# The end of the global attention and the second output product: order by token halves, a weight split moved, the last tile in halves

## The chip, the cores and the metric

One core of a Trainium2 chip runs one layer in one launch. The metric is the device time in microseconds: three timed runs of the kernel before gave 1565.99, 1567.54 and 1567.87, median 1567.54. Engines: PE (TensorE, matmuls, and PEld, its weight loads), DVE (VectorE), ACT (ScalarE), POOL (GpSimd), SP (SyncE, which here issues nearly all DMAs).

## The reference

One layer over 1024 tokens of width 1024, with 256 context tokens. Two attention branches run side by side, A windowed and B global, each with 8 query heads of 64 and 2 key heads; their outputs are merged through gates, projected and added to the stream, and a convolutional SwiGLU follows.

```
h = x * (1 + scale1) + shift1
q, k, v, gate_logits = h @ w_in + b_in             # rotary, RMS norm on q and k of B
o_a = windowed_attention(...); o_b = global_attention(...)     # softmax over keys and context
g_a, g_b = split(sigmoid(gate_logits))
y = (g_a * (o_a @ w_branch_a) + g_b * (o_b @ w_branch_b)) @ w_out
x = layer_norm(alpha * x + gate1 * y)
x = layer_norm(alpha * x + gate2 * conv_ffn(x * (1 + scale2) + shift2))
```

The change touches the end of `o_b`, the product `o_b @ w_branch_b` and the merge ahead of `w_out`.

## The kernel before, in words

All tensors are float32, and PE multiplies in a rounded 32-bit form. To keep precision each operand is **split** into a high part (a rounded copy, "h") and a low part (the difference, "l"); a product is then three matmuls (`mm3`, lines 88 to 91: high by high, high by low, low by high). The function `split` (lines 80 to 86) makes the two parts, each on an engine that the caller names.

The stages in order: modulation and projections (to about 330 us), the 16 units of branch A (to 485), the 16 units of branch B (to 757), the output product of B with the merge (to 805), `w_out` and the first LayerNorm (to about 885), the FFN's up tiles (to 1330), its down tiles (to 1552) and the last LayerNorm.

**A unit** is 128 queries of one key group, with four heads side by side: a name such as `1_7_1` is branch 1 (B), query tile 7, group 1, the last of all. After its softmax come the value steps: for each of ten key tiles n PE transposes the probabilities (`ptr`, L613), the result is split into `pth` and `ptl`, and two matmuls add to `av` (L634, L635). The split is made by ACT (cast, L622) and DVE (subtraction, L623); for the key tiles in `POOL_LO`, 2 and 6 of branch B, ACT copies to `prw` (L619) and POOL makes both parts (L83, L86), and the matmuls of such a tile are queued one place later (`PLAG`). When `av` is complete, `out_step` copies it to `avs` (ACT, L640), moves its upper half down (`up`, POOL, L642), adds the halves (`ot`, L646: POOL in branch B, DVE in A), multiplies by the broadcast reciprocal of the softmax sums (`rb`, L649, POOL) and splits into the `O` tiles (POOL, L83 and L86).

**The output product of B** has eight tiles f of 128 channels by 1024 tokens, each for two token halves of 512 (hf). Half 0 is made of query tiles 0 to 3, half 1 of 4 to 7, so only half 1 needs the last unit. A half is 12 matmuls, 24 a tile. Its weight comes in four pieces for two tiles each (`wb`), each loaded into `rwb` and split into `hwb` and `lwb`. Tiles 0 and 1 are made by `branch_steps` (L947 evicts with the gate as factor into `bT1_f`), four groups in the order (0, half 0), (0, half 1), (1, half 0), (1, half 1), in the PSUM tiles `pt` of the attention, one bank each. Tiles 2 to 7 follow in a loop of their own (evicted at L1086), each in a `big` tile of two banks; there are three such buffers. Tile 2 needs the weight piece `wb[1]`, which is loaded and split after tiles 0 and 1. The function `merge` adds the tile to that of branch A (L1067, DVE), casts (`mh`, ACT) and subtracts (`ml`, DVE). Then `w_out`'s product y reads `mh` and `ml` (first y: tokens 0 to 511), again in `big` tiles, as do the first up tiles of the FFN, named u0_j and u1_j.

After up tile 2 the `big` tiles are given up, and the up tiles from 3 on use the eight PSUM banks singly, in a fixed order of banks (`PSU` = 6, 7, 2, 3, 4, 5, 0, 1) for a, b, c, d of each tile. So the third bank in use is one that a `big` tile held, and its first matmul waits until that tile's last reader is done.

The order on PE is the order of the code. On ACT, DVE and POOL the compiler's scheduler may move instructions, except inside `manual_schedule`, where the code's order holds. Each engine takes its queue in order, and so does SP with its DMAs.

Of the kernel before, what the change touches and what calls it, by code (L numbers as in the profile page):

```python
# [68 lines left out]
def layer_kernel(  # L69
# [393 lines left out]
    class Unit:  # L463
# [141 lines left out]
        def value_steps(self):  # L605
            nm, kt = self.id, self.kt
            vh = self.br * 2 + self.g
            parts = {}

            def tr_step(n):  # L610
                tr = pt_tile(f"ptr{nm}_{n}")
                for h in range(4):
                    nc.tensor.transpose(tr[:, h * P:(h + 1) * P], self.pslice(h, n), ident)  # L613
                hi = att.tile([P, 512], R32, tag="pth", name=f"pth{nm}_{n}", bufs=4)
                lo = att.tile([P, 512], R32, tag="ptl", name=f"ptl{nm}_{n}", bufs=4)
                pooled = n in POOL_LO[self.br]
                if pooled:
                    rw = att.tile([P, 512], F32, tag="ptr", name=f"prw{nm}_{n}", bufs=2)
                    nc.scalar.copy(rw, tr)  # L619
                    split(rw, hi, lo, nc.gpsimd, nc.gpsimd)  # L620
                else:
                    nc.scalar.copy(hi, tr)  # L622
                    nc.vector.tensor_tensor(out=lo, in0=tr, in1=hi.bitcast(F32), op=ALU.subtract)  # L623
                parts[n] = hi, lo
                return pooled

            def av_step(n):
                first = self.left == len(kt)
                self.left -= 1
                if first:  # L630
                    self.av = ps2.tile([P, 512], F32, tag="av", name=f"av{nm}")
                hi, lo = parts.pop(n)
                v = VT[kt[n] // 2][:, kt[n] % 2, vh]
                nc.tensor.matmul(self.av, v, hi, start=first, stop=False)  # L634
                nc.tensor.matmul(self.av, v, lo, start=False, stop=self.left == 0)  # L635

            def out_step():
                av = self.av
                avs = att.tile([P, 512], F32, tag="ptr", name=f"avs{nm}", bufs=2)
                nc.scalar.copy(avs, av)  # L640
                up = att.tile([HD, 512], F32, tag="up", name=f"up{nm}", bufs=1)
                nc.gpsimd.tensor_scalar(out=up, in0=avs[HD:P], scalar1=1.0, scalar2=0.0, op0=ALU.mult, op1=ALU.add)  # L642
                ot = att.tile([P, 2, P], F32, tag="ot", name=f"ot{nm}", bufs=1)
                oe = nc.gpsimd if self.br else nc.vector
                for h in range(2):
                    oe.tensor_tensor(out=ot[h * HD:(h + 1) * HD],  # L646
                                     in0=avs[0:HD].rearrange("p (a b q) -> p a b q", b=2, q=P)[:, :, h],
                                     in1=up.rearrange("p (a b q) -> p a b q", b=2, q=P)[:, :, h], op=ALU.add)
                nc.gpsimd.tensor_tensor(out=ot, in0=ot, in1=self.rb, op=ALU.mult)  # L649
# [247 lines left out]
    def s_tile(name):  # L897
        return ps2.tile([P, T], F32, tag="s", name=name, bufs=2)

    def p_tile(name):  # L900
        return att.tile([P, T], F32, tag="p", name=name, bufs=8)

# [21 lines left out]
    def branch_steps(br, wsrc, halves, wpool, engs, f2s=range(4)):  # L924
# [24 lines left out]
        for f2 in f2s:  # L949
            steps.append(lambda f2=f2: ld(f2, f"{f2}_{halves[0]}"))  # L950
            for f in (2 * f2, 2 * f2 + 1):
                for hf in halves:
                    steps.append(lambda f=f, hf=hf: grp(f, hf, pt_tile))
        return steps

    def done(br, i, g):
# [40 lines left out]
    nc.sync.dma_start(cvw, conv)  # L997
    nc.sync.dma_start(cvb, convb)
    hput("KC", *[f"VT{t}" for t in range(5)])
    for st_ in first[1:]:  # L1000
        st_()
    ps2.release()
    att.release()
    qp.release()
# [13 lines left out]

    def sml(name, w=512):
        return ps3.tile([P, w], F32, tag="sml", name=name, bufs=2)  # L1020

    def weight(src, nm, n=8, tag="w", he=None, le=None, rtag="raw"):
        if rtag:
            r = post.tile([P, 8, P], F32, tag=rtag, name=f"r{nm}", bufs=3)[:, 0:n]
        else:
            r = ht(f"r{nm}", (P, n, P))
            hput(f"r{nm}")
        nc.sync.dma_start(r, src)
        if tag is None:
            h, l = (ht(f"{a}{nm}", (P, n, P), R32) for a in "hl")  # L1030
        else:
            pool = wq if tag == "w" else post
            h, l = (pool.tile([P, 8, P], R32, tag=tag, name=f"{a}{nm}", bufs=4)[:, 0:n] for a in "hl")
        split(r, h, l, he or nc.gpsimd, le or nc.gpsimd)
        return h, l

    def hsl(hf):
        return slice(hf * HALF, (hf + 1) * HALF)
# [23 lines left out]
            nc.sync.dma_start(z, xT[f][:, hsl(hf)])  # L1062
            nc.gpsimd.tensor_scalar(out=z, in0=z, scalar1=ALPHA, scalar2=0.0, op0=ALU.mult, op1=ALU.add)

    def merge(f):
        m = bT[0, f]
        nc.vector.tensor_tensor(out=m, in0=m, in1=bT[1, f], op=ALU.add)  # L1067
        mh, ml = ht(f"mh{f}", dt=R32), ht(f"ml{f}", dt=R32)
        split(m, mh, ml, nc.scalar, nc.vector)
        hput(f"bT0_{f}", f"bT1_{f}")  # L1070
        mrg.append((mh, ml))

    for f in (0, 1):
        merge(f)
    wb = {f2: weight(w_b[f2], f"wb{f2}", 8, he=nc.scalar, le=nc.vector, rtag=None) for f2 in (1, 2)}
    for f in range(2, KT):
        bT[1, f] = ht(f"bT1_{f}")
        nc.sync.dma_start(bT[1, f], sgd[KT + f])
        w = wb[f // 2]
        ps = big(f"b1_{f}")  # L1080
        for j in range(4):
            k = (f % 2) * 4 + j
            for hf in (0, 1):
                a = O[1, hf, 0, j // 2][:, j % 2], O[1, hf, 1, j // 2][:, j % 2]
                mm3(ps[:, hsl(hf)], (w[0][:, k], w[1][:, k]), a, j == 0, j == 3)
# [823 lines left out]
```

## Time and profile before

| | before |
|---|---|
| timed runs, us | 1565.99, 1567.54, 1567.87 |
| profiled execution, us | 1568.55 |
| its span, first to last instruction, us | 1566.8 |
| mean granted TensorE clock | 0.995 |

Busy time is what the profile counts between start and end of an instruction, so overlapping matmuls leave a busy PE even where they start later than they could. In the rows of the timeline the columns are start, duration, engine, line, operation, output and inputs, shape, and in brackets the engine's idle time before it and the instruction that ended it. In the rows by stretch the columns are busy time and number of instructions on PE, PEld, DVE, ACT and POOL, the granted clock of PE, the share of DMA engines busy and the GB/s.

### The profile page before, as it was taken

What the parts mean: (1) busy time and instruction counts of PE and PEld (TensorE: products, weight loads), DVE (VectorE), ACT (ScalarE), POOL (GpSimd) and SP (SyncE); (2) the same over time, 40 slices, a digit from 0 to 9 for tenths busy, and PEclk for the clock granted to TensorE, in tenths of its full rate; (3) what the DMA queues carried; (4) which work ended last, traced back from release to release, by engine and by line L of the source; (5) the groups of instructions that cost most, each with busy time, mean ns of one, the idle gap of its engine ahead of it and who ended that gap; (6) DMA issues with size and microseconds to landing.
All of it is one profiled execution on the core that took longest, in us unless ns stands there. A gap on an engine that the chain in (4) does not pass through costs nothing.

```text
span 1566.8 us, 22288 instructions
## 1 busy us (share of the span) xinstructions
PE 1533.8 (98%) x7804; PEld 1283.3 (82%) x7804; DVE 1187.2 (76%) x1707; ACT 808.2 (52%) x1430; POOL 788.7 (50%) x801
## 2 busy tenths in 40 slices
PE   9999999999999999999999999999999999999997
PEld 7888888888877878877788998888888888888887
DVE  6676976548887777778573789888888888657884
ACT  5323223358887777777330574544444444435552
POOL 0356423526667777776442445766677774021121
PEclk9999999999999999999999999999999999999998
DMA  9776662322236666631550223233334446996721
GB/s 370 263 245 238 210 239 93 109 82 64 65 118 142 143 161 148 142 75 32 180 178 24 82 91 112 93 108 109 121 108 112 113 115 187 365 269 208 254 103 55
DMA packets 113105, 232.11 MB, mean 148 GB/s; under 512 B 13056, under 2 KB 27904, under 8 KB 112896
## 3 DMA queue, kind: packets, MB, share of 16 engines
q1 hardware_dynamic: 97760, 201.82, 38.2%
q0 software_dynamic: 10400, 20.19, 8.3%
q10 hardware_dynamic: 4832, 8.68, 1.5%
q8 instruction: 61, 1.00, 0.3%
q14 instruction: 52, 0.43, 0.1%
HBM read 179.45 MB, written 65.86 MB: 157 GB/s over the span
## 4 chain that ended last, share of the span: by engine, by line
PE 56%; DVE 2%; ACT 1%; issue 0%; POOL 0%; DVEq 0%; ACTq 0%
PE p L91 4%; PE p L89 4%; PE p L90 4%; PE b L91 3%; PE b L89 2%; PE b L90 2%; PE c L89 2%; PE a L89 2%; PE d L89 2%; PE d L91 2%; PE a L90 2%; PE c L90 2%; PE d L90 2%; PE a L91 2%; PE c L91 2%; PE y L90 2%
## 5 line engine op out<-in xcount | busy, mean ns | idle before, releaser
L623 DVE TENSOR_TENSOR ptl<-ptr,pth 128x512 fp32r<-128x512 f32 x188 | 124.9, 683 | 32.5 <-ACT pth L622 32.1
L622 ACT CAST pth<-ptr 128x512 fp32r<-128x512 f32 x188 | 106.8, 592 | 52.7 <-PE ptr L613 31.2
L86 DVE TENSOR_TENSOR ld<-rd,hd 128x1024 fp32r<-128x1024 f32 x77 | 95.9, 1264 | 50.0 <-ACT hd L81 47.9
L505 ACT ACTIVATE p<-p,nm 128x1024 f32<-128x1024 f32 (+2 forms) x128 | 125.9, 985 | 4.6 <-DVE p L538 4.3
L613 PE MATMUL ptr<-ident,p 128*128 128x128 f32 x816 | 122.2, 276 | 4.4 <-DVE ptl L623 3.2
L81 ACT CAST hd<-rd 128x1024 fp32r<-128x1024 f32 x77 | 79.4, 1050 | 81.5 <-PE p L91 51.3
L613 PEld LDWEIGHTS ptr<-ident,p 128*128 128x128 f32 x816 | 94.0, 140 | 25.7 <-DVE ptl L623 7.7
L86 POOL TENSOR_TENSOR wlg<-wg,whg 128x512 fp32r<-128x512 f32 x32 | 46.5, 1462 | 123.6 <-ACT whg L81 123.3
L634 PE MATMUL av<-pth,VT 128*128 128x512 f32 x236 | 104.4, 442 | 2.7 <-ACT avs L640 1.5
L89 PE MATMUL p<-hd 128*128 128x512 f32 x264 | 103.4, 392 | 0.0
L91 PE MATMUL p<-hd,ld 128*128 128x512 f32 x264 | 102.9, 390 | 0.0
L90 PE MATMUL p<-ld,hd 128*128 128x512 f32 x264 | 102.9, 390 | 0.0
L635 PE MATMUL av<-ptl,VT 128*128 128x512 f32 x236 | 98.3, 416 | 3.5 <-POOL ptl L86 3.5
L89 PE MATMUL g<-hh,whg 128*128 128x512 f32 x256 | 100.0, 391 | 0.0
L91 PE MATMUL g<-hh,wlg 128*128 128x512 f32 x256 | 99.8, 390 | 0.0
L90 PE MATMUL g<-hl,whg 128*128 128x512 f32 x256 | 99.7, 390 | 0.0
L538 DVE TENSOR_SCALAR_CACHE_REDUCE p<-s,cvt,nmc 128x1024 f32<-128x1024 f32 x64 | 83.2, 1316 | 8.7 <-PE s L494 7.6
L493 PE MATMUL s<-KL,q 128*128 128x512 f32 (+2 forms) x192 | 75.8, 395 | 5.5 <-ACT p_x L505 2.8
L494 PE MATMUL s<-KL,q 128*128 128x512 f32 (+2 forms) x192 | 71.6, 373 | 0.0
L786 ACT ACTIVATE sg<-g,bgc 128x512 f32<-128x512 f32 x32 | 22.0, 686 | 96.1 <-PE g L91 96.1
L81 ACT CAST wS<-s 128x512 fp32r<-128x512 f32 x76 | 45.3, 620 | 45.3 <-POOL s L1211 44.6
L81 ACT CAST wA<-ru 128x512 fp32r<-128x512 f32 x57 | 35.5, 623 | 63.7 <-PE d L91 34.9
(436 smaller groups left out, 5030.2 us busy)
## 6 DMA issues: line engine op xcount, KB each, us to landing
wml<-in_wmodT_dram SPq DMA_DIRECT2D x48, 512.0 KB
ru<-in_w_up_dram SPq DMA_DIRECT2D x38, 512.0 KB
rd<-td SPq DMA_DIRECT2D x55, 256.0 KB
rd<-sd SPq DMA_DIRECT2D x44, 256.0 KB
rd<-in_w_dn_dram SPq DMA_DIRECT2D x33, 256.0 KB
wm<-in_wmodT_dram SPq DMA_DIRECT2D x16, 512.0 KB
wg<-in_w_g_dram SPq DMA_DIRECT2D x32, 256.0 KB
sgd<-sg ACTq DMA_DIRECT2D x32, 256.0 KB
```

Source lines behind the costliest of these rows:

```text
L81: nc.scalar.copy(hi, src)
L86: lo_eng.tensor_tensor(out=lo, in0=src, in1=hi.bitcast(F32), op=ALU.subtract)
L89: nc.tensor.matmul(ps, a[0], b[0], start=start, stop=False, skip_group_check=resumed)
L90: nc.tensor.matmul(ps, a[0], b[1], start=False, stop=False, skip_group_check=resumed)
L91: nc.tensor.matmul(ps, a[1], b[0], start=False, stop=stop, skip_group_check=resumed)
L505: nc.scalar.activation(p, s, AF.Exp, bias=nm[:, h:h + 1], scale=scale, accum_out=sm[:, h:h + 1])
L538: nc.vector.tensor_scalar(out=p, in0=o, scalar1=self.qscale(nqs)[:, hs] if self.br else -1.0, scalar2=self.other[:, hs], op0=ALU.mult, op1 ...
L613: nc.tensor.transpose(tr[:, h * P:(h + 1) * P], self.pslice(h, n), ident)
L622: nc.scalar.copy(hi, tr)
L623: nc.vector.tensor_tensor(out=lo, in0=tr, in1=hi.bitcast(F32), op=ALU.subtract)
L634: nc.tensor.matmul(self.av, v, hi, start=first, stop=False)
L635: nc.tensor.matmul(self.av, v, lo, start=False, stop=self.left == 0)
```

## The change

Four edits, in one diff:

1. In the last unit no key tile is split on POOL, and its `ot` is added on DVE.
2. The groups of tiles 0 and 1 are called in the order (0, half 0), (1, half 0), (0, half 1), (1, half 1), and the last of them takes an `s` tile of PSUM, not a `pt`.
3. `wb[1]` is called between the first and the second group, inside a `manual_schedule` of DVE and ACT with them; its buffers are given back after tile 3. The function `weight` moves up with it, as do the lines that follow it unchanged.
4. Tile 7 is computed, evicted and merged in two halves, in `sml` tiles of PSUM in place of a `big` one.

```diff
@@ value_steps, tr_step, out_step
+            last = self.id == f"1_{NT - 1}_1"
...
-                pooled = n in POOL_LO[self.br]
+                pooled = n in POOL_LO[self.br] and not last
...
-                oe = nc.gpsimd if self.br else nc.vector
+                oe = nc.gpsimd if self.br and not last else nc.vector
...
+    def s_half(name):
+        return s_tile(name)[:, 0:HALF]
...
@@ branch_steps
                 for hf in halves:
-                    steps.append(lambda f=f, hf=hf: grp(f, hf, pt_tile))
+                    mk = s_half if br and f % 2 and hf else pt_tile
+                    steps.append(lambda f=f, hf=hf, mk=mk: grp(f, hf, mk))
...
-    for st_ in first[1:]:
-        st_()
+    wb = {}
+    with tc.manual_schedule(engines={mybir.EngineType.DVE, mybir.EngineType.Activation}):
+        first[1]()
+        wb[1] = weight(w_b[1], "wb1", 8, tag=None, he=nc.scalar, le=nc.vector, rtag=None)
+        for n in (3, 2, 4):
+            first[n]()
...
-    def merge(f):
+    def merge(f, parts=(slice(0, T),)):
         m = bT[0, f]
-        nc.vector.tensor_tensor(out=m, in0=m, in1=bT[1, f], op=ALU.add)
         mh, ml = ht(f"mh{f}", dt=R32), ht(f"ml{f}", dt=R32)
-        split(m, mh, ml, nc.scalar, nc.vector)
+        for s in parts:
+            nc.vector.tensor_tensor(out=m[:, s], in0=m[:, s], in1=bT[1, f][:, s], op=ALU.add)
+            split(m[:, s], mh[:, s], ml[:, s], nc.scalar, nc.vector)
...
-    wb = {f2: weight(w_b[f2], f"wb{f2}", 8, he=nc.scalar, le=nc.vector, rtag=None) for f2 in (1, 2)}
+    wb[2] = weight(w_b[2], "wb2", 8, he=nc.scalar, le=nc.vector, rtag=None)
...
-        ps = big(f"b1_{f}")
-        for j in range(4):
-            k = (f % 2) * 4 + j
-            for hf in (0, 1):
-                a = O[1, hf, 0, j // 2][:, j % 2], O[1, hf, 1, j // 2][:, j % 2]
-                mm3(ps[:, hsl(hf)], (w[0][:, k], w[1][:, k]), a, j == 0, j == 3)
-        nc.vector.tensor_tensor(out=bT[1, f], in0=ps, in1=bT[1, f], op=ALU.mult)
-        merge(f)
+        halves = [(0, 1)] if f < KT - 1 else [(0,), (1,)]
+        for hs in halves:
+            n = HALF * len(hs)
+            b = bT[1, f][:, hs[0] * HALF:hs[0] * HALF + n]
+            ps = big(f"b1_{f}") if len(hs) == 2 else sml(f"b1_{f}_{hs[0]}")
+            for j in range(4):
+                k = (f % 2) * 4 + j
+                for m, hf in enumerate(hs):
+                    a = O[1, hf, 0, j // 2][:, j % 2], O[1, hf, 1, j // 2][:, j % 2]
+                    mm3(ps[:, hsl(m)], (w[0][:, k], w[1][:, k]), a, j == 0, j == 3)
+            nc.vector.tensor_tensor(out=b, in0=ps, in1=b, op=ALU.mult)
+        merge(f, [slice(hs[0] * HALF, (hs[-1] + 1) * HALF) for hs in halves])
         if f == 3:
+            hput("hwb1", "lwb1")
             wb[3] = weight(w_b[3], "wb3", 8, he=nc.scalar, le=nc.vector, rtag=None)
```

Below the first edit the lines of the changed kernel are one higher than before, in the output product some four to sixteen.

What stands on POOL at the end of the last two units (`_7_0_` and `_7_1_`), before:

```order
L83 TENSOR_SCALAR pth1_7_1_2_8635<-prw1_7_1_2_8637 128x512
L642 TENSOR_SCALAR up1_7_0_8654<-avs1_7_0_8652 64x512
L86 TENSOR_TENSOR ptl1_7_1_2_8636<-prw1_7_1_2_8637,pth1_7_1_2_8635 128x512
L646 TENSOR_TENSOR ot1_7_0_8656<-avs1_7_0_8652,up1_7_0_8654 64x256 x2
L649 TENSOR_TENSOR ot1_7_0_8656<-ot1_7_0_8656,rb1_7_0_8537 128x256
L83 TENSOR_SCALAR O1100_7333<-ot1_7_0_8656 128x2x128
L86 TENSOR_TENSOR O1110_7334<-ot1_7_0_8656,O1100_7333 128x2x128
L83 TENSOR_SCALAR pth1_7_1_6_8698<-prw1_7_1_6_8700 128x512
L86 TENSOR_TENSOR ptl1_7_1_6_8699<-prw1_7_1_6_8700,pth1_7_1_6_8698 128x512
L642 TENSOR_SCALAR up1_7_1_8749<-avs1_7_1_8747 64x512
L646 TENSOR_TENSOR ot1_7_1_8751<-avs1_7_1_8747,up1_7_1_8749 64x256 x2
L649 TENSOR_TENSOR ot1_7_1_8751<-ot1_7_1_8751,rb1_7_1_8687 128x256
```

and on POOL now:

```order
L643 TENSOR_SCALAR up1_7_0_8652<-avs1_7_0_8650 64x512
L647 TENSOR_TENSOR ot1_7_0_8654<-avs1_7_0_8650,up1_7_0_8652 64x256 x2
L650 TENSOR_TENSOR ot1_7_0_8654<-ot1_7_0_8654,rb1_7_0_8537 128x256
L83 TENSOR_SCALAR O1100_7333<-ot1_7_0_8654 128x2x128
L86 TENSOR_TENSOR O1110_7334<-ot1_7_0_8654,O1100_7333 128x2x128
L643 TENSOR_SCALAR up1_7_1_8745<-avs1_7_1_8743 64x512
L650 TENSOR_TENSOR ot1_7_1_8747<-ot1_7_1_8747,rb1_7_1_8687 128x256
L83 TENSOR_SCALAR O1101_7566<-ot1_7_1_8747 128x2x128
L86 TENSOR_TENSOR O1111_7567<-ot1_7_1_8747,O1101_7566 128x2x128
```

The four splits of key tiles 2 and 6 and the last unit's two additions are gone from POOL; the first go to ACT and DVE, the additions to DVE.

What stands on DVE from the last subtraction of the attention on (`bT1_f` are evictions and then merges into `bT0_f`), before:

```order
L623 TENSOR_TENSOR ptl1_7_1_9_8734<-ptr1_7_1_9_8728,pth1_7_1_9_8733 128x512
L947 TENSOR_TENSOR bT1_0_8759<-b1_0_0_8761,bT1_0_8759 128x512
L947 TENSOR_TENSOR bT1_0_8759<-b1_0_1_8776,bT1_0_8759 128x512
L1067 TENSOR_TENSOR bT0_0_5576<-bT0_0_5576,bT1_0_8759 128x1024
L947 TENSOR_TENSOR bT1_1_8790<-b1_1_0_8792,bT1_1_8790 128x512
L86 TENSOR_TENSOR ml0_8835<-bT0_0_5576,mh0_8834 128x1024
L947 TENSOR_TENSOR bT1_1_8790<-b1_1_1_8807,bT1_1_8790 128x512
L1067 TENSOR_TENSOR bT0_1_5717<-bT0_1_5717,bT1_1_8790 128x1024
L86 TENSOR_TENSOR lwb1_8846<-rwb1_8843,hwb1_8845 128x1024
L86 TENSOR_TENSOR lwb2_8852<-rwb2_8849,hwb2_8851 128x1024
L86 TENSOR_TENSOR ml1_8840<-bT0_1_5717,mh1_8839 128x1024
L1086 TENSOR_TENSOR bT1_2_8855<-b1_2_8857,bT1_2_8855 128x1024
```

and now:

```order
L624 TENSOR_TENSOR ptl1_7_1_9_8730<-ptr1_7_1_9_8724,pth1_7_1_9_8729 128x512
L647 TENSOR_TENSOR ot1_7_1_8747<-avs1_7_1_8743,up1_7_1_8745 64x256 x2
L951 TENSOR_TENSOR bT1_0_8757<-b1_0_0_8759,bT1_0_8757 128x512
L86 TENSOR_TENSOR lwb1_8776<-rwb1_8773,hwb1_8775 128x1024
L951 TENSOR_TENSOR bT1_1_8779<-b1_1_0_8781,bT1_1_8779 128x512
L951 TENSOR_TENSOR bT1_0_8757<-b1_0_1_8796,bT1_0_8757 128x512
L1079 TENSOR_TENSOR bT0_0_5576<-bT0_0_5576,bT1_0_8757 128x1024
L951 TENSOR_TENSOR bT1_1_8779<-b1_1_1_8811,bT1_1_8779 128x512
L86 TENSOR_TENSOR ml0_8839<-bT0_0_5576,mh0_8838 128x1024
L1079 TENSOR_TENSOR bT0_1_5717<-bT0_1_5717,bT1_1_8779 128x1024
L86 TENSOR_TENSOR lwb2_8851<-rwb2_8848,hwb2_8850 128x1024
L86 TENSOR_TENSOR ml1_8844<-bT0_1_5717,mh1_8843 128x1024
```

`lwb1` has moved six rows up, ahead of the second group's eviction, and `ot` has come in. Its high part, `hwb1`, now stands on ACT directly behind `avs1_5_1`, the output of the unit four before the last, and its load on SP where the loads of `bT1_1` stood (issued at 621.69 in the profile); those two loads now stand around the row `dn1_7_0`, which is issued at 739.66.

The third place is on PE in the up tile 3, the first that uses single banks, where b ends and c begins. Before:

```order
L90 MATMUL b3_10538<-T24l_3_10328,wS2_3_10528 128x512
L91 MATMUL b3_10538<-T24h_3_10327,wS2_3_10528 128x512
L89 MATMUL c3_10539<-T13h_0_10254,wS1_3_10531 128x512 [waits PE_49]
L90 MATMUL c3_10539<-T13l_0_10255,wS1_3_10531 128x512
L91 MATMUL c3_10539<-T13h_0_10254,wS1_3_10531 128x512
```

and now:

```order
L90 MATMUL b3_10542<-T24l_3_10332,wS2_3_10532 128x512
L91 MATMUL b3_10542<-T24h_3_10331,wS2_3_10532 128x512
L89 MATMUL c3_10543<-T13h_0_10258,wS1_3_10535 128x512 [waits DVE_49,Activation_49]
L90 MATMUL c3_10543<-T13l_0_10259,wS1_3_10535 128x512
L91 MATMUL c3_10543<-T13h_0_10258,wS1_3_10535 128x512
```

The instructions are the same; the wait of c3's first matmul is another. Before, it was for PE's last matmul into u0_2; now it is for the readers of u1_2, the convolution on ACT (L1371 before) and DVE (L1374 before).

More of the change, by code (lines that the diff above doesn't have):

```diff
@@ L999, in layer_kernel @@
     hput("KC", *[f"VT{t}" for t in range(5)])
-    for st_ in first[1:]:
-        st_()
-    ps2.release()
-    att.release()
-    qp.release()
-    za = tc.alloc_tile_pool(name="za", bufs=1, side="right", reuse_waits="tile")
-    wq = tc.alloc_tile_pool(name="wq", bufs=1, side="right", reuse_waits="tile")
-    ps3 = tc.alloc_tile_pool(name="ps3", bufs=1, space=PSUM, reuse_waits="tile")
-    hfree += [(za, f"Z{n}") for n in range(16)]
-    def tm(name, dt=F32, w=T):
-        return post.tile([P, w], dt, tag="m", name=name, bufs=4)
-    def big(name):
-        return ps3.tile([P, T], F32, tag="big", name=name, bufs=3)
-    def sml(name, w=512):
-        return ps3.tile([P, w], F32, tag="sml", name=name, bufs=2)
     def weight(src, nm, n=8, tag="w", he=None, le=None, rtag="raw"):
@@ L1035, in weight, with tm, big, sml @@
         return h, l
+    wb = {}
[4 more added lines that the diff above has]
+            first[n]()
+    ps2.release()
+    att.release()
+    qp.release()
+    za = tc.alloc_tile_pool(name="za", bufs=1, side="right", reuse_waits="tile")
+    wq = tc.alloc_tile_pool(name="wq", bufs=1, side="right", reuse_waits="tile")
+    ps3 = tc.alloc_tile_pool(name="ps3", bufs=1, space=PSUM, reuse_waits="tile")
+    hfree += [(za, f"Z{n}") for n in range(16)]
+    def tm(name, dt=F32, w=T):
+        return post.tile([P, w], dt, tag="m", name=name, bufs=4)
+    def big(name):
+        return ps3.tile([P, T], F32, tag="big", name=name, bufs=3)
+    def sml(name, w=512):
+        return ps3.tile([P, w], F32, tag="sml", name=name, bufs=2)
     def hsl(hf):
```

## The prediction

> **What bounds the kernel now.** I read the page's busy table and slices first, then the windows by stage, then the PE timeline around the end of the attention, where the change works.
>
> ```profile
> span 1566.8 us, 22288 instructions
> PE 1533.8 (98%) x7804; PEld 1283.3 (82%) x7804; DVE 1187.2 (76%) x1707; ACT 808.2 (52%) x1430; POOL 788.7 (50%) x801
> PE 56%; DVE 2%; ACT 1%; issue 0%; POOL 0%; DVEq 0%; ACTq 0%
> 864.00:1552.00 688.00, 688.00 (x3360) 583.13 (x3359) 556.49 (x590) 344.78 (x472) 331.27 (x211) 1.00 0.47 146
> ```
>
> TensorE sets the time. From 864 to 1552 it is busy in all 688 us, so work that reaches that stretch earlier ends earlier by as much, unless something new stops PE there. Within busy time a matmul can still start late, so I count starts, not busy shares. The pace when nothing waits:
>
> ```profile
> 764.18 0.39 PE L91 MATMUL b<-O,lwb 128*128 128x512 f32 x1
> ...
> 769.62 0.39 PE L91 MATMUL b<-O,lwb 128*128 128x512 f32 x1
> ```
>
> These are the first and last of 25 rows: 5.44 us for 24 steps, **0.2267 us a matmul**. Everything below is start time lost against that pace. The sum is made against the profiled execution (1568.55 us, span 1566.8), which is 1.01 above the median of the three timed runs (1567.54, from 1565.99 to 1567.87); I move the median by the sum.
>
> **Part 1, key tiles 2 and 6 of the last unit.** The timeline of the unit's end:
>
> ```profile
> 753.62 0.39 PE L635 MATMUL av<-ptl,VT 128*128 128x512 f32 x1
> 753.99 0.61 POOL L83 TENSOR_SCALAR pth<-prw 128x512 fp32r<-128x512 f32 x1
> 754.65 0.50 PE L634 MATMUL av<-pth,VT 128*128 128x512 f32 x1 [0.65 <-POOL pth L83]
> 754.68 1.27 POOL L86 TENSOR_TENSOR ptl<-prw,pth 128x512 fp32r<-128x512 f32 x1
> 756.00 0.50 PE L635 MATMUL av<-ptl,VT 128*128 128x512 f32 x1 [0.85 <-POOL ptl L86]
> 757.74 0.63 PE L89 MATMUL b<-O,hwb 128*128 128x512 f32 x1
> ```
>
> PE waits twice for the split of tile 6, which POOL begins only at 753.99. After the row at 753.62 six more value matmuls follow, then the first b matmul: at pace 753.62 + 7 x 0.2267 = 755.2. The change takes POOL out. ACT keeps its count (a cast in place of a copy), and DVE gets two subtractions more:
>
> ```profile
> 752.46 2.20 DVE L623 TENSOR_TENSOR ptl<-ptr,pth 128x512 fp32r<-128x512 f32 x3 [1.02 <-ACT pth L622]
> ```
>
> One of the two falls into DVE's idle 1.02 us before this row (a subtraction is 0.61 to 0.73 here, the row's 2.20 being three); the other moves the last lo part from 754.66 to about 755.3, its matmul to 755.4 and the first b to 755.7. So the first b starts between 755.2 and 755.7; I take 755.4, **2.35 us earlier**.
>
> **Part 2, the slow clock.** Just after that wait the granted clock falls:
>
> ```profile
> 757.00:758.00 1.00, 1.00 (x4) 0.81 (x3) 0.00 (x0) 0.00 (x0) 0.00 (x0) 0.50 0.90 328
> ...
> 759.00:760.00 1.00, 1.00 (x4) 0.78 (x3) 0.00 (x0) 0.00 (x0) 0.92 (x2) 0.50 0.99 393
> 763.16 0.19 PEld L90 LDWEIGHTS b<-O,hwb 128*128 128x128 f32 x1 [0.22 <-POOL O L86]
> ```
>
> The 48 b matmuls run from 757.74 to 769.62: 11.88 us for 47 steps, against 10.65 at pace. **1.23 us** are lost, nearly all to the clock of 0.50, some 0.07 to the weight load that waited for the last unit's output. With the wait of part 1 gone the drop has no cause left here, and I count all of it.
>
> That output comes sooner as well. It now goes ACT, POOL, DVE, POOL:
>
> ```profile
> 758.04 0.59 ACT L640 COPY avs<-av 128x512 f32<-128x512 f32 x1 [4.10 <-PE av L635]
> 758.78 0.61 POOL L642 TENSOR_SCALAR up<-avs 64x512 f32<-64x512 f32 x1 [2.83 <-ACT avs L640]
> 761.06 0.73 POOL L649 TENSOR_TENSOR ot<-ot,rb 128x256 f32<-128x256 f32 x1
> 761.88 0.41 POOL L83 TENSOR_SCALAR O<-ot 128x256 fp32r<-128x256 f32 x1
> 762.37 0.74 POOL L86 TENSOR_TENSOR O<-ot,O 128x256 fp32r<-128x256 f32 x1
> L646 DVE TENSOR_TENSOR ot<-avs,up x32: 385/418/861, 353.5 to 484.1; 64x256 f32<-64x256 f32 x32
> ```
>
> From 755.7: 0.59 + 0.61 + 2 x 0.42 + 0.73 + 0.41 + 0.74 = 3.92, and some 0.1 at each of five handovers: done at about 760.1. By the new order of groups PE needs it at b matmul 31, not 19: 755.4 + 30 x 0.2267 = 762.2. So 2 us are spare. The one thing I can't place is when the broadcast reciprocal (rb) lands, which the multiply needs; it was there by 761.06, and were it that late again, the low part would come at 763.0 and PE would lose 0.6 to 0.8. Bounds 0 and 0.8; I take 0, since it is issued 7 us ahead.
>
> The new row on DVE right behind is the subtraction lwb1, both operands in SBUF, beside POOL's last three rows. [...]
>
> **Part 3, the wait ahead of b1_2 and its weight.** The next rows in time:
>
> ```profile
> 770.05 0.69 DVE L947 TENSOR_TENSOR bT<-b,bT 128x512 f32<-128x512 f32 x1 [0.89 <-PE b L91]
> 770.89 0.47 PE L89 MATMUL b<-O,hwb 128*128 128x512 f32 x1 [0.88 <-DVE bT L947]
> 771.92 2.77 DVE L86 TENSOR_TENSOR lwb<-rwb,hwb 128x1024 fp32r<-128x1024 f32 x2
> 773.19 0.51 PE L91 MATMUL b<-O,lwb 128*128 128x512 f32 x1 [0.90 <-DVE lwb L86]
> 804.83 0.39 PE L89 MATMUL y<-mh,hwo 128*128 128x512 f32 x1
> ```
>
> From 769.62 to the first y matmul lie 145 steps (six tiles of 24, and one): 32.87 at pace, 35.21 measured, **2.35 lost**, at the two waits. In the changed order b1_2 waits for the eviction of group (1, first half), two groups earlier; and lwb1 is done by about 760.3 for a need at 766.7. Both go. DVE's next deadline is b1_5, at 782.6, which needs the eviction of b1_2; DVE reaches that behind seven operations of 0.7 to 1.4 us from 766.5, by some 775. 7 us spare.
>
> The cast hwb1 goes into ACT's queue far ahead of this:
>
> ```profile
> 698.10 0.63 ACT L640 COPY avs<-av 128x512 f32<-128x512 f32 x1
> 701.18 1.20 ACT L622 CAST pth<-ptr 128x512 fp32r<-128x512 f32 x2 [2.45 <-PE ptr L613]
> 768.50 1.04 ACT L81 CAST hwb<-rwb 128x1024 fp32r<-128x1024 f32 x1
> 621.69 1.02 SPq L940 DMA_DIRECT2D bT<-sgd  x2
> ```
>
> It takes 1.04 of 2.45 us idle, and its data is asked for where bT1_1's loads stood, at 622. Those loads move to about 741 on SP, between rows that wait longer themselves; they are needed at 763. Nothing on the path.
>
> **Part 4, the last tile in halves.**
>
> ```profile
> 810.03 0.19 PEld L90 LDWEIGHTS y<-ml,hwo 128*128 128x128 f32 x1 [0.47 <-DVE ml L86]
> ```
>
> Here a weight load of y waited for ml of the last tile, 0.47 us; the matmul starts around it lose **0.3 us** against pace. The first y uses the first half of the tokens alone, whose product now ends 12 matmuls (2.7 us) sooner and is evicted, merged and split in half-size steps, so the wait goes. The halves cost DVE some 0.4 us more (0.69 twice for 1.22, and the like), beside idle DVE.
>
> **Part 5, what comes back.** b1_7 no longer takes one of the three `big` buffers, so u1_2 later lands in another one. When the buffers turn into banks, the third bank (c of the next tile) lies in u1_2's, no longer in u0_2's:
>
> ```profile
> 974.61 0.39 PE L89 MATMUL c<-T13h,wS 128*128 128x512 f32 x1
> 973.97 1.27 DVE L1374 SCALAR_TENSOR_TENSOR c<-u,cvt,c 128x1023 f32<-128x1023 f32 x1
> 936.64 1.23 DVE L86 TENSOR_TENSOR lwu<-rwu,hwu 128x1024 fp32r<-128x1024 f32 x1 [1.85 <-PE u L90]
> ```
>
> c's first matmul started at 974.61; the convolution that reads u1_2 ended at 975.24, and PE follows DVE by about 0.15 (770.74 to 770.89 above). That is a **new wait of 0.78 us**, if DVE moves with PE. It does: DVE runs nearly without a gap up to here from 936.64, where it waited for PE. Bounds: 0 (DVE gets 0.8 ahead in the calmer stretch before) and 7 (DVE doesn't move at all).
>
> **The sum.** 2.35 + 1.23 + 2.35 + 0.3 - 0.78 = 5.45 us. Profiled: 1568.55 - 5.45 = 1563.1; median: **1562.1**.
>
> **Rivals.**
>
> *The clock decides otherwise.* A second slow stretch follows the LN statistics, where PE runs one-column products:
>
> ```profile
> 756.89 0.63 PE L634 MATMUL av<-pth,VT 128*128 128x512 f32 x1
> ...
> 852.85 0.38 PE L1160 MATMUL sta<-onec,zs 128*128 128x1 f32 x2
> ...
> 855.82 0.63 PE L89 MATMUL y<-mh,hwo 128*128 128x512 f32 x1
> ...
> 856.00:864.00 8.00, 8.00 (x27) 5.76 (x26) 2.83 (x6) 0.59 (x1) 0.90 (x1) 0.81 0.01 2
> ```
>
> If a drop of the size of part 2 still comes near the last unit, 1.2 us are not won: 1563.3. If the one at 856 goes away, 0.19 x 8 = 1.5 us more are won: 1560.6. For it: two drops, each after thin work of some 3 us; against it: at 770 to 773 PE started only seven matmuls and no drop followed. [...]
>
> *The last unit is paced by DVE.* If both added subtractions count in full (2 x 0.68), the last lo part ends at 756.0, the first b at 756.4; PE then still thins out there and the drop of 1.2 remains: 1.0 + 1.2 less, 1564.3. For it: DVE is busy 2.20 us without a gap at the end. Against it: 1.02 idle just before.
>
> *The change does its part and c3 takes it back.* If DVE's chain to 975.24 keeps its place, c3 waits for 975.39 while PE is there at 968.2: all is lost, 1568.3. Against it: the wait for PE at 936.64.
>
> *Slower.* ACT takes its queue in order, and hwb1 stands ahead of the casts of unit 1_6_0. If its data hadn't landed, every later cast would wait, and PE with it. It decides from 700.1 (698.73 + 2.45 - 1.04) on, us for us; for a loss of 0.2% it would have to land past 708.7, having been issued near 622: 1571 and more.
>
> **How the numbers follow.** Forecast 0.62, clock 0.20 (half each way), DVE-paced 0.09, c3 0.06, ACT's queue 0.03. A measurement of this kernel can tell about 0.2%, 3.1 us: faster means below 1564.4. Faster 0.62 + 0.20 + half of the DVE case, which lies on the bound: 0.86. Same 0.11, slower 0.03. The range takes in the clock case below with half of the timed runs' spread (1560.6 - 1.0) and the DVE case above with as much (1564.3 + 0.9): 1559.6 to 1565.2.
>
> **What would show it.** Right: no idle time before the av matmuls with POOL named; first b near 755.4; clock 1.00 in 756 to 761; b's 48 starts 10.7 long; no wait before b1_2; first y near 798.9; c3's first matmul with some 0.8 idle, DVE named. Wrong: a new wait in the value matmuls with DVE or ACT named, a wait for POOL's O in the second half groups, an idle PE between 864 and 1552 other than at c3, or ACT standing at 699.

## The result and the profile after

The changed kernel takes **1563.85 us** (median of 8 runs, 1561.96 to 1565.27) against 1568.3 for the kernel before beside it (8 runs, 1565.52 to 1570.73): 4.45 us less, ratio 0.9971 with the interval 0.9962 to 0.9979. The profiled execution of the changed kernel took 1565.22, so it is one of the longer ones.

From the page after: the span, the busy table and the last chain by engine. They say little more than that TensorE still sets the time.

```profile
span 1563.4 us, 22286 instructions
PE 1531.6 (98%) x7804; PEld 1282.2 (82%) x7804; DVE 1187.6 (76%) x1714; ACT 808.6 (52%) x1431; POOL 782.2 (50%) x795
PE 54%; DVE 3%; ACT 1%; issue 1%; POOL 0%; DVEq 0%; ACTq 0%
```

The windows after, columns as in the prediction:

```profile
756.00:760.00 4.00, 4.00 (x20) 3.29 (x19) 1.57 (x4) 0.59 (x1) 1.60 (x3) 1.00 0.79 233
864.00:1552.00 688.00, 686.25 (x3366) 581.62 (x3365) 550.68 (x583) 343.40 (x471) 326.55 (x208) 1.00 0.47 146
```

The clock behind the last unit is 1.00 where it was 0.50 (the rows 757 to 760 of the prediction). From 864 to 1552 TensorE now stands for 1.75 us, all in one place, as the timeline of PE shows:

```profile
738.10 0.51 PE L635 MATMUL av<-pth,VT 128*128 128x512 f32 x1 [0.29 <-ACT avs L641]
...
755.41 0.40 PE L635 MATMUL av<-pth,VT 128*128 128x512 f32 x1
...
756.34 0.39 PE L89 MATMUL b<-O,hwb 128*128 128x512 f32 x1
...
767.00 0.39 PE L91 MATMUL b<-O,lwb 128*128 128x512 f32 x1
...
799.86 0.39 PE L89 MATMUL y<-mh,hwo 128*128 128x512 f32 x1
...
969.06 0.39 PE L91 MATMUL b<-T24h,wS 128*128 128x512 f32 x1
971.20 0.47 PE L89 MATMUL c<-T13h,wS 128*128 128x512 f32 x1 [1.75 <-DVE c L1390]
```

The first row is a place that the change doesn't touch: a value matmul of the last unit but one. The same row of the kernel before:

```profile
737.11 0.51 PE L634 MATMUL av<-pth,VT 128*128 128x512 f32 x1 [0.29 <-ACT avs L640]
```

So this execution of the changed kernel was 0.99 us late already at this row. Most of that came between 480 and 500, where its granted clock had dropped (0.69 in the row 484 to 488, 0.89 in the next): there it went from 0.52 us ahead of the kernel before to 0.80 behind. The loads and the cast that the change moves ahead of this row can account for the other 0.19 at most. Times that are compared below are therefore counted from this row in each trace, which I call the mark. Four stretches hold the change from there on:

| stretch, us | before | after | gain | forecast |
|---|---|---|---|---|
| mark to first b | 20.63 | 18.24 | 2.39 | 2.35 |
| first to last of the 48 b matmuls | 11.88 | 10.66 | 1.22 | 1.23 |
| last b to first y | 35.21 | 32.86 | 2.35 | 2.35 |
| first y to first c of the fourth tile | 169.78 | 171.34 | -1.56 | 0.3 - 0.78 = -0.48 |
| sum | 237.50 | 233.10 | 4.40 | 5.45 |

Three terms come out to a few hundredths. The fourth is 1.08 worse, and that is the gap between 5.45 and the 4.40 of these two traces. The medians' 4.45 agrees, but each trace is one execution, so two digits of agreement are chance.

The last unit's output after, on ACT, POOL and DVE, in three fences:

```profile
756.54 0.59 ACT L641 COPY avs<-av 128x512 f32<-128x512 f32 x1 [1.49 <-PE av L636]
```

```profile
757.29 0.61 POOL L643 TENSOR_SCALAR up<-avs 64x512 f32<-64x512 f32 x1 [3.67 <-ACT avs L641]
758.92 0.74 POOL L650 TENSOR_TENSOR ot<-ot,rb 128x256 f32<-128x256 f32 x1 [1.02 <-DVE ot L647]
759.75 0.41 POOL L83 TENSOR_SCALAR O<-ot 128x256 fp32r<-128x256 f32 x1
760.24 1.58 POOL L86 TENSOR_TENSOR O<-ot,O 128x256 fp32r<-128x256 f32 x1
```

```profile
757.93 0.85 DVE L647 TENSOR_TENSOR ot<-avs,up 64x256 f32<-64x256 f32 x2 [2.17 <-POOL up L643]
759.87 1.35 DVE L86 TENSOR_TENSOR lwb<-rwb,hwb 128x1024 fp32r<-128x1024 f32 x1
```

The multiply by `rb` starts right behind DVE's `ot`, so the reciprocal had landed. The low part takes 1.58 in place of 0.74, beside `lwb`, and ends at 761.82; b matmul 31 starts at 756.34 + 30 x 0.2267 = 763.14, 1.3 us later, and doesn't wait. The row grew by 0.84 us, inside those 1.3. In `wb_late` below, where `lwb` stands elsewhere, the same row takes 0.74.

### The profile page after: what moved, and what is told of

It is laid out like the page before. It is cut to its first block, busy times and chain, and to the rows that moved or that the text cites. A ratio compares the mean times of both kernels' runs of the same rounds, so it can differ in the third digit from the quotient of the medians.

```text
span 1563.4 us, 22286 instructions
## 1 busy us (share of the span) xinstructions
PE 1531.6 (98%) x7804; PEld 1282.2 (82%) x7804; DVE 1187.6 (76%) x1714; ACT 808.6 (52%) x1431; POOL 782.2 (50%) x795
## 2 busy tenths in 40 slices
DMA packets 113105, 232.11 MB, mean 148 GB/s; under 512 B 13056, under 2 KB 27904, under 8 KB 112896
## 4 chain that ended last, share of the span: by engine, by line
PE 54%; DVE 3%; ACT 1%; issue 1%; POOL 0%; DVEq 0%; ACTq 0%
PE p L89 4%; PE p L90 4%; PE p L91 4%; PE b L89 2%; PE b L91 2%; PE b L90 2%; PE c L89 2%; PE c L91 2%; PE d L91 2%; PE d L89 2%; PE c L90 2%; PE d L90 2%; PE a L91 2%; PE a L89 2%; PE a L90 2%; PE y L91 2%
```

## The experiments

Twelve runs, in three batches; each batch has its own runs of the kernel before (medians 1568.43, 1569.11 and 1568.28). In each expectation A is the account that I held when I wrote it (in the first ones the prediction's, later corrected by earlier runs); other letters are rivals.

### The wait at c: the same bank order, with and without the change

The bank order is turned so that c no longer takes the bank of u1_2 (`c3_bank`, changed kernel), and the same edit is made in the kernel before, where it should bring the wait in (`before_c3`).

```diff
-PSU = 6, 7, 2, 3, 4, 5, 0, 1
+PSU = 6, 7, 0, 1, 4, 5, 2, 3
```

> The changed kernel, with the fixed order of PSUM banks of the up tiles from 3 on set to 6, 7, 0, 1, 4, 5, 2, 3, so that c of tile 3 lies in the banks of u0_2 again and not in those of u1_2. Theory A (all that the forecast missed is the wait at c3, 1.91 us in the profile of the changed kernel: 0.78 forecast and 1.11 because a DVE multiplication took 2.33 us there in place of 1.22): c3's first matmul follows b's last without idle time, nothing later takes it back, and the time is 0.8 to 1.9 us under the changed kernel's: 1562 to 1563 beside 1563.9, a ratio to before near 0.996. Theory B (DVE is behind at this place whatever the banks are, so the next wait of PE takes the gain): c3 starts at once, PE waits within the next 30 us for DVE instead, and the time is that of the changed kernel, ratio 0.997.

> The kernel before, with the bank order 6, 7, 0, 1, 4, 5, 2, 3, so that c of tile 3 lies in u1_2's banks as in the changed kernel; nothing else. Theory A: a wait of 0.8 us at c3 where the multiplication on DVE ahead of it takes 1.2 us, as it did in the profile of before, or 1.9 where it takes 2.3; the run 0.8 to 1.9 us slower than before, ratio 1.0005 to 1.0012. Theory B (the wait is only there because DVE falls behind by what the change adds to it): no idle time at c3, ratio 1.000.

`c3_bank`: 1562.56 us, ratio 0.9961 (0.9948 to 0.9973). `before_c3`: 1570.58, ratio 1.001 (1.0001 to 1.0019). Timelines of PE, first `c3_bank`, then `before_c3`:

```profile
966.94 0.39 PE L89 MATMUL c<-T13h,wS 128*128 128x512 f32 x1
```

```profile
976.88 0.47 PE L89 MATMUL c<-T13h,wS 128*128 128x512 f32 x1 [0.64 <-DVE c L1374]
```

The wait goes with the banks in the one and comes with them in the other: its cause is shown. Rival B expected PE to wait for DVE soon after instead; in `c3_bank` PE is busy in all 578.06 us from 966.94 to 1545. The size of the wait is not the same: 0.64 idle here, which with the late first start is 0.8, and 1.75 in the changed kernel. The difference lies on DVE and POOL some 7 to 10 us earlier. The changed kernel, DVE then POOL:

```profile
961.64 2.33 DVE L1399 TENSOR_TENSOR c<-c,c 128x1024 f32<-128x1024 f32 x1
```

```profile
961.61 1.28 POOL L86 TENSOR_TENSOR wS<-s,wS 128x512 fp32r<-128x512 f32 x1 [2.43 <-ACT wS L81]
```

And the kernel before, DVE then POOL:

```profile
966.96 1.22 DVE L1383 TENSOR_TENSOR c<-c,c 128x1024 f32<-128x1024 f32 x1
```

```profile
966.93 2.40 POOL L86 TENSOR_TENSOR wS<-s,wS 128x512 fp32r<-128x512 f32 x1 [2.44 <-ACT wS L81]
```

The same pair, started 0.03 us apart in both profiles. One of the two takes 1.22 (DVE) or 1.28 (POOL), the other about 1.1 longer than that. In the changed kernel's profile it was DVE, and c came 1.1 later: DVE has one gap from there to c, 0.40 us for ACT, and ACT had itself waited for DVE's step behind the multiplication. That gave a test.

### No POOL operation beside the gate multiplication

`s4_dve`, changed kernel: the low part of that one weight tile is made on DVE. If the POOL row beside it is what stretches the multiplication, it should be short here.

```diff
-            split(wsrc.pop((j, n)), t[:, 0], t[:, 1], nc.scalar, getattr(nc, UE[list(prods).index(n)]))
+            split(wsrc.pop((j, n)), t[:, 0], t[:, 1], nc.scalar,
+                  nc.vector if (j, n) == (3, "S4") else getattr(nc, UE[list(prods).index(n)]))
```

> The changed kernel with the low part of weight tile 3 of the fourth up product made on VectorE, so that GpSimd does no subtraction from SBUF beside the gate multiplication ahead of c's first matmul of the fourth tile. [...] Ratio 0.9965 to 0.9975 by A.

1562.51 us, ratio 0.9966 (0.9955 to 0.9977). Timelines of DVE and of PE:

```profile
959.73 1.21 DVE L1399 TENSOR_TENSOR c<-c,c 128x1024 f32<-128x1024 f32 x1
```

```profile
968.28 0.47 PE L89 MATMUL c<-T13h,wS 128*128 128x512 f32 x1 [0.73 <-DVE c L1390]
```

With no POOL row beside it the multiplication is short, 1.21, and c waits 0.73. One profile can't prove that 2.33 never comes here. Over the 13 profiles that have the pair, DVE was the one stretched in 4 (2.33 or 2.34) and POOL in 9 (2.39 or 2.40), one of the kernel before in the first group among them. The traces in which c lies in u1_2's banks say more. In the five where POOL was the one stretched c waits 0.62 to 0.64 (`before_c3`, `no_last`, `no_last_again`, `pt_all`, `order_old`); in the two where DVE was, 1.75 in both (the changed kernel and `wb_late`). So c's loss is about 0.8 in most executions and 1.9 in the others. The kernel before doesn't go free either: in the two traces with the old bank of c and DVE stretched (`before_again2`, `part1_only`) PE stands 0.50 us at a later c, at 982.85 and 981.75.

### Part 1: POOL back in the last unit, and part 1 alone

`no_last` is the changed kernel with POOL splitting tiles 2 and 6 of the last unit and adding `ot` as before; it was profiled a second time as `no_last_again`. `part1_only` is the kernel before with the first edit alone.

```diff
-            last = self.id == f"1_{NT - 1}_1"
+            last = False
```

> The changed kernel without its first edit: key tiles 2 and 6 of the last unit split on POOL and the unit's output added on POOL, as before. Theory A (the POOL wait cost 2.4 us and the clock drop that it brings another 1.2): PE waits for POOL's parts of tile 6 again, the first b matmul 2.4 us later against the rest, the clock near 0.5 for some 3 us behind it, and the last unit's output 3 us later, within what the group order spares; 2.4 to 3.6 us slower than the changed kernel, ratio to before 0.9986 to 0.9994. [...]

> The kernel before with the first edit alone: the last unit's key tiles 2 and 6 split on ACT and DVE, its output added on DVE. Theory A (the wait for POOL and the clock drop behind it go together, 2.4 and 1.2): 3.6 us faster than before, ratio 0.9977. [...]

`no_last`: 1566.4 us, ratio 0.9984 (0.9975 to 0.9993), so taking part 1 away costs 0.0013 x 1568 = 2.0 us by the medians, though the two intervals overlap. PE there:

```profile
751.68 0.51 PE L635 MATMUL av<-pth,VT 128*128 128x512 f32 x1 [0.67 <-POOL pth L83]
753.03 0.50 PE L636 MATMUL av<-ptl,VT 128*128 128x512 f32 x1 [0.84 <-POOL ptl L86]
754.29 0.39 PE L89 MATMUL b<-O,hwb 128*128 128x512 f32 x1
```

The mark stands at 734.13, so the first b is at 20.16, against 18.24 after: 1.92, with the clock at 1.00 throughout.

`part1_only`: 1568.84 us, ratio 0.9996 (0.9987 to 1.0005). I had not expected this. The first b comes at mark + 18.24 as in the changed kernel (the mark stands at 737.52), and then PE, POOL and SP's queue read:

```profile
762.00 0.49 PE L89 MATMUL b<-O,hwb 128*128 128x512 f32 x1 [2.00 <-POOL O L83]
762.81 0.50 PE L90 MATMUL b<-O,hwb 128*128 128x512 f32 x1 [0.32 <-POOL O L86]
```

```profile
760.73 0.72 POOL L650 TENSOR_TENSOR ot<-ot,rb 128x256 f32<-128x256 f32 x1 [3.40 <-DMA rb<-dn]
```

```profile
752.30 0.33 SPq L1029 DMA_DIRECT2D rwb<-in_w_b_dram  x1
752.72 0.28 SPq L586 DMA_DIRECT2D dn<-rb  x1
754.10 0.33 SPq L1079 DMA_DIRECT2D bT<-sgd  x1
756.98 1.53 SPq L588 DMA_DIRECT2D rb<-dn  x2
```

The gain of 1.92 goes straight into a wait for the output, which is held by the reciprocal. It takes two DMAs, `dn<-rb` and then `rb<-dn`. The second is issued only at 756.98, mark + 19.46. A load of `bT` stands ahead of it, but that had left SP by 754.43; the next 2.5 us SP waits for the first DMA to land, and the first had been issued late, at mark + 15.20, behind both weight loads (750.24 and 752.30). In the kernel before one of these loads stands behind it, and the two go out at mark + 13.82 and mark + 16.49:

```profile
750.93 0.27 SPq L586 DMA_DIRECT2D dn<-rb  x1
751.33 0.33 SPq L1028 DMA_DIRECT2D rwb<-in_w_b_dram  x1
753.60 1.24 SPq L588 DMA_DIRECT2D rb<-dn  x2
```

In the changed kernel neither weight load stands ahead of them there, and they go out at mark + 14.69 and mark + 15.90:

```profile
752.79 0.27 SPq L586 DMA_DIRECT2D dn<-rb  x1
754.00 1.24 SPq L588 DMA_DIRECT2D rb<-dn  x2
```

So the order on SP in `part1_only` is neither the old one nor the new one. POOL's multiply starts 4.97 us after the first b, against 2.58 in the changed kernel, so the wait for the output comes mainly from that order. In the changed kernel part 1 is worth the 1.92 by these traces; what it would win alone with the old order on SP no run shows.

### Was part 2 the clock? More profiles of the kernel before

> The kernel before, unchanged, profiled once more to see whether the slow clock after the last unit belongs to the wait for GpSimd. Theory A (the thin stretch of value matmuls causes the drop each time): some 4-us stretch between 752 and 768 at a granted clock below 0.85, and the first b matmul to the first y matmul 47.1 us. Theory C (a matter of the run): in some executions no such drop, and then 45.9 us, 1.2 less. Of three profiles with that wait so far two show the drop, one does not.

> The same kernel and the same question once more: Theory A 47.1 us from the first b to the first y with a clock below 0.85 in 752 to 768; Theory C 45.9 us without it in some of the profiles.

> The changed kernel with GpSimd still splitting two tiles of the last unit, profiled once more. Theory A: the drop follows the wait, first y some 1.2 us later relative to the first b than the 43.52 of its first profile (44.7). Theory C: the drop comes in some executions and not in others, 43.5 or 44.7.

1567.58, 1568.81 and 1562.69 us, one run each, which say nothing by themselves. The windows of the first two, `before_again1` and then `before_again2`:

```profile
756.00:760.00 4.00, 4.00 (x19) 3.29 (x19) 0.56 (x1) 0.59 (x1) 2.25 (x4) 1.00 0.92 333
```

```profile
756.00:760.00 4.00, 4.00 (x13) 3.13 (x12) 0.00 (x0) 0.59 (x1) 1.92 (x3) 0.62 0.95 351
772.00:776.00 4.00, 3.63 (x9) 2.92 (x10) 3.42 (x3) 1.21 (x2) 2.31 (x2) 0.59 0.35 128
```

No drop in the one, two drops in the other: C, a matter of the run. But the numbers that both theories gave were wrong for the first: from the first b to the first y it takes 47.08 us without a drop. PE in `before_again1`, with no drop:

```profile
756.52 0.39 PE L89 MATMUL b<-O,hwb 128*128 128x512 f32 x1
...
761.10 0.50 PE L89 MATMUL b<-O,hwb 128*128 128x512 f32 x1 [0.34 <-POOL O L83]
761.91 0.50 PE L90 MATMUL b<-O,hwb 128*128 128x512 f32 x1 [0.31 <-POOL O L86]
...
768.39 0.39 PE L91 MATMUL b<-O,lwb 128*128 128x512 f32 x1
...
803.60 0.39 PE L89 MATMUL y<-mh,hwo 128*128 128x512 f32 x1
```

768.39 - 756.52 = 11.87, the same as the 11.88 with the drop. At full clock PE reaches the matmul that needs the last unit's output before it is there, and loses to the output what it would have lost to the clock: POOL ends the low part 5.34 us after the first b here and 5.37 in the first profile of before (762.37 + 0.74 to 757.74). In `no_last_again`, where POOL's wait is there, no drop follows and the groups stand in the new order, the 48 starts take 767.14 - 756.47 = 10.67 (to the first y 43.54, as its C had it); in `order_old` below, with the old order and the clock at 1.00, they take 12.01. So the 1.2 us are the wait for the output, and it is **the order of the groups that removes it, not the clock**. The first profile of `no_last` had said the same, and I had read it as "no drop this time".

Where nothing lies beside it a drop does cost: the second drop of `before_again2` makes its stretch from last b to first y 36.80 (768.81 to 805.61) in place of 35.21. After the last unit the clock dropped in 3 of the 4 profiles of kernels with POOL's wait in the old group order, in neither of the two with the wait in the new one, and in none of the 8 without the wait. These counts are small: they suggest that the wait favours a drop, and no more. Both profiles of `no_last` are short executions besides (1562.31, the lowest of its 11, and 1562.69, against a median of 1566.4), so they may have missed drops that others had.

### Part 3 in pieces

Three edits of the changed kernel: all groups in `pt` tiles (`pt_all`), the old order of groups (`order_old`), and wb[1] called behind all groups (`wb_late`).

```diff
-                    mk = s_half if br and f % 2 and hf else pt_tile
+                    mk = pt_tile
```

> The changed kernel with all four groups of the first two tiles in pt tiles, none in an s tile; order and weight as changed. Theory A (the wait ahead of b1_2 came from the PSUM buffer of the last group, not from the order of the groups): b1_2's first matmul waits for the last group's eviction again, 0.9 to 1.1 us, the rest as in the changed kernel; 1 us slower than it, ratio to before 0.9977. Theory D (the order alone took the wait away): no wait, ratio 0.9971.

```diff
-        for n in (3, 2, 4):
+        for n in (2, 3, 4):
```

> The changed kernel with the four groups in the old order (0, half 0), (0, half 1), (1, half 0), (1, half 1); the weight between the first two and the s tile for the last group as changed. Theory A (the order only spares the last unit's output, whose low part came at 761.8 in the changed kernel's profile against a need at 763.1, and would be needed at 760.7): a wait of 0.9 to 1.2 us for POOL's low part inside the second group, none ahead of b1_2; 1 us slower than the changed kernel, ratio 0.9977. Rival F (the order also holds the wait ahead of b1_2): waits at both places, 2 us slower, ratio 0.9984.

```diff
-        wb[1] = weight(w_b[1], "wb1", 8, tag=None, he=nc.scalar, le=nc.vector, rtag=None)
         for n in (3, 2, 4):
             first[n]()
+        wb[1] = weight(w_b[1], "wb1", 8, tag=None, he=nc.scalar, le=nc.vector, rtag=None)
```

> The changed kernel with the second weight piece called behind the four groups (still inside the fixed order of DVE and ACT), the rest as changed. Theory A (the split's place was worth the wait of 0.9 ahead of the third matmul of b1_2): a wait of 0.8 to 1.2 us there for lwb1, and the low part of the last unit's output no longer stretched by the subtraction beside it (0.74 us in place of 1.58); 1 us slower than the changed kernel, ratio 0.9977. Rival G (with the loads issued as early as now, ACT and DVE have the weight ready in time anyway): no wait, ratio 0.9971.

The new wait of each (of `wb_late` the first of three), from PE's timeline, in the order of the edits:

```profile
766.24 0.50 PE L89 MATMUL b<-O,hwb 128*128 128x512 f32 x1 [0.79 <-DVE bT L951]
```

```profile
762.59 0.50 PE L90 MATMUL b<-O,hwb 128*128 128x512 f32 x1 [1.04 <-POOL O L86]
```

```profile
767.83 0.50 PE L89 MATMUL b<-O,hwb 128*128 128x512 f32 x1 [0.33 <-DVE bT L951]
```

In `wb_late` the row names the eviction, and two weight loads behind it wait 0.27 us each, for `hwb` and for `lwb`; the expectation had one wait of 0.8 to 1.2 for `lwb1` alone, and why the eviction is named stays open. The first y, counted from the mark, comes at 62.90, 63.11 and 62.64, against 61.76 after: 1.14, 1.35 and 0.88 us later. The times can't tell them from the changed kernel: ratios 0.9968 (0.9957 to 0.998), 0.9961 (0.9946 to 0.9977, four runs) and 0.9973 (0.9963 to 0.9982); `order_old` even came out lower. The traces say which wait each piece removes. In `pt_all` the order of groups is the new one and the wait ahead of b1_2 is back, and in `order_old` it is absent with the old order: that wait is removed by the `s` tile of the last group, not by the order, to which the prediction put it down. `order_old` also prices the order itself: 1.35 us, for the last unit's output.

### The halves

`whole7`: the changed kernel with tile 7 in one piece.

```diff
-        halves = [(0, 1)] if f < KT - 1 else [(0,), (1,)]
+        halves = [(0, 1)]
```

> The changed kernel without its last edit: tile 7 in one big tile, evicted and merged whole. Theory A (the halves win 0.3 at the first y and cost 0.8 at c3 by the bank that moves): a wait of 0.3 to 0.5 at the first y's last inputs, none at c3, 0.5 us faster than the changed kernel, ratio to before 0.9965 to 0.9969. Rival E (the halves were needed more than the trace of before shows, since PE now comes sooner to y against the same DVE chain): a wait of 1 us or more at y, as slow as the changed kernel or slower.

1564.16 us, ratio 0.997 (0.9961 to 0.9979). PE and DVE:

```profile
806.49 0.50 PE L89 MATMUL y<-mh,hwo 128*128 128x512 f32 x1 [0.76 <-ACT mh L81]
808.01 0.50 PE L90 MATMUL y<-ml,hwo 128*128 128x512 f32 x1 [1.01 <-DVE ml L86]
```

```profile
802.43 1.21 DVE L1101 TENSOR_TENSOR bT<-b,bT 128x1024 f32<-128x1024 f32 x1
```

c has no wait here, as tile 7 takes a `big` buffer again, so the partner to compare with is `c3_bank`, neither with a drop of the clock behind the mark up to c: c at mark + 231.91 against 229.58. The halves are worth **2.3 us**, not 0.3. With the earlier waits gone PE begins y at 800.81, and DVE starts to evict tile 7 only 1.62 us after that; in the kernel before it did so 0.20 after (805.03 to 804.83). So `whole7` loses 2.3 at y and saves c's wait, and the change loses c's wait and saves the 2.3; in time they can't be told apart. `c3_bank` has both.

## Why the prediction was right, point by point

- **Bound by TensorE, counted in starts.** Held: all gains are starts that came earlier, and 688 - 686.25 = 1.75 us at c is all that was given back behind 864.
- **Part 1, 2.35.** The row measures 2.39, for the path that the prediction describes (first b at mark + 18.24; 755.4 forecast from a mark of 737.11 is 18.29). But 0.47 of it was slow clock inside the last value matmuls; the wait for POOL is worth 1.92 in an execution without it (mark to first b 20.15 in `before_again1`, 20.16 and 20.17 in the two of `no_last`). And it is worth it only if the output keeps up: `part1_only`, with its late reciprocal, kept nothing that the times can show.
- **Part 2, 1.23.** Size right at 1.22, cause wrong, so the size was luck: the change happened to hold the remedy for the true cause as well. The step "nearly all to the clock of 0.50, some 0.07 to the weight load that waited" read the 0.07 as the whole price of the output. It was only what was left of it beside the slow clock; without a drop the output takes all of the 1.2. The group order was counted as nothing of its own and earned it. The rival on the clock (1.2 not won if a drop still comes) was priced from the same wrong cause: in the kernel before, a drop there costs the 0.47 inside the value matmuls, and not 1.2 more. What one would cost there in the new order no trace shows; the drop with nothing beside it cost 1.59 (36.80 - 35.21). Of the signs named against a drop, PE starts five matmuls from 770 to 773, not seven, which changes no term.
- **rb.** Taken as 0, between 0 and 0.8: 0 in the changed kernel. `part1_only` shows that it can matter: with another order on SP, and the old order of groups, the reciprocal held a wait of 2 us.
- **Part 3, 2.35.** Measured 2.35, at the two places named. One reason was wrong: "in the changed order b1_2 waits for the eviction of group (1, first half)" credits the order, and the `s` tile did it. The pieces cost 1.14 without the `s` tile and 0.88 with the weight late, 2.02 together.
- **Part 4, 0.3.** The wait of the kernel before was sized rightly, but it is not the price of the edit: without the halves the same place would now cost 2.3. The step left out that a later engine falls behind once earlier waits go. The sum doesn't suffer, since the halves were in.
- **Part 5, -0.78.** This is the mis-sized term. Place, cause and direction held (`c3_bank`, `before_c3`), and 0.8 is what most executions lose. The profile after lost 1.9, since DVE's gate multiplication was the one that was stretched. With the 4 in 13 seen here the mean is 0.8 + 1.1 x 4/13 = 1.1, an estimate from few traces.
- **The sum.** 5.45 forecast. By the first profile of before it is 4.40; by `before_again1`, with no drop at the last unit, 237.24 - 233.10 = 4.14; by `s4_dve`, where c waits 0.73, 237.24 - 232.11 = 5.13. The medians say 4.45, by the ratio's interval 3.3 to 6.0, which holds 5.45 too: the times alone don't show that anything is missing. By the traces the rest is likely the larger mean loss at c (0.3) and the part-1 clock that not every execution had (up to 0.5); this split is argued, not shown. The forecast of 1562.1 was counted down from 1567.54, and beside the changed kernel the kernel before took 1568.3, which is the other 0.76 of the 1.75 between 1562.1 and 1563.85.
- **Rivals.** DVE did not pace the last unit (before no value matmul of it does PE stand idle for DVE or POOL), c did not take all back, and `hwb1` did not hold ACT's queue, as ACT's timeline after shows: the cast is done by 700.56, and the next one still stands idle for PE.

```profile
699.47 1.09 ACT L81 CAST hwb<-rwb 128x1024 fp32r<-128x1024 f32 x1
702.09 1.22 ACT L623 CAST pth<-ptr 128x512 fp32r<-128x512 f32 x2 [1.52 <-PE ptr L614]
```

## What to carry to other kernels

A slow clock or a short wait may be the cover of a later wait: before pricing it, ask when the next operand would have been there at full speed. Gains in a row are not separate sums: one edit alone won nothing here, and another that removed 0.3 us kept 2.3 from coming back once the others were in. Before an edit is blamed for winning nothing, compare the order of every queue with the kernel it came from; here the DMA queue's had changed. When buffers change hands, follow the buffers to the next stage that reuses them; turning the bank order (`c3_bank`) took c's wait away and gave the lowest c of all traces, and with a ratio of 0.9961 it is faster than the kernel before and, by the trace, than the changed one, though the two ratios' intervals overlap.

## What the runs showed of the hardware that I had not expected

The pair of DVE and POOL rows that starts 0.02 to 0.04 us apart comes out one way or the other: 1.22 and 2.40, or 2.33 and 1.28, in one and the same kernel (kernel before: the first in two profiles, the second in one). The stretched row is 1.1 longer, about the length of the other (1.22 or 1.28). The recorded order alone doesn't say which it is: POOL's row starts first in all 13 profiles, and in 9 of them POOL is the one stretched. How far it leads nearly does: 25 to 28 ns in eight of these nine and 32 in the ninth (`before_c3`), 29 to 36 in the four where DVE is stretched, so one exception in 13. What decides it in the engines no trace shows. c stands behind this pair without slack: it waited 0.64 us in `before_c3`, where POOL was stretched, and 1.75 in the changed kernel, where DVE was.

Drops of the granted clock come at other places in each execution. In the stretch of LN statistics (848 to 860), which the change doesn't touch, 8 of 14 profiles show one. In the clock records of the traces each drop before the last stage lasts 3.41 us at 0.50, and drops of one trace start whole multiples of that apart: 98.99 us or 29.0 times in the kernel before (756.69 and 855.68), 17.07 us or 5.0 times in `before_again2` (755.62 and 772.69). What sets their place no run shows. The same thin work may or may not have a drop behind it, as the two profiles of the unchanged kernel above show: none after the last unit in `before_again1`, two in `before_again2`. A microsecond between two single profiles is for that reason no evidence in this kernel; starts counted between two fixed rows are, where no drop lies between them.
